# Sums of squares of an SSD chunk: folded to one block of 128 columns, and taken two chunks later by one matmul

## The chip, the cores and the metric

One core of one Trainium2 chip runs the whole program. The time is device microseconds (us) of one execution; lower is better. The kernel before was run three times: 2429.6, 2432.8 and 2435.5 us, median 2432.8.

## What is computed

One layer of a hybrid recurrent decoder for a prompt of 1,024 tokens behind 16 meta tokens, and eight samples of 4 tokens. One of its two branches is a state-space scan (SSD), run in chunks of 128 tokens, with 32 heads of 64 features in 4 groups. Its output is gated and then normalised over the 512 features of a group:

```python
y = jnp.concatenate(ys, axis=1) + w['D'].astype(f32)[:, None] * xs.astype(f32)
y = y.reshape(Bsz, L, S_INNER) * jax.nn.silu(z.astype(f32))
yg = y.reshape(Bsz, L, S_GROUPS, S_INNER // S_GROUPS)
yg = yg * lax.rsqrt(jnp.mean(jnp.square(yg), -1, keepdims=True) + RMS_EPS)
```

The change concerns `jnp.mean(jnp.square(yg), -1)`: for each token, a sum of squares over 512 features.

## The kernel before, in words

**Layout.** In the SSD stage features lie on the 128 partitions and tokens along the columns. A chunk of one group is a tile `xc` of 128 x 10 x 128: four blocks of 128 features of x, then B, C, and four blocks of the gate z. The first chunk has 48 tokens (samples and meta tokens), the eight others 128.

**Order of the work.** `ssd(g)` returns the steps of one group: `first`; `sample` and `sample_states` for the samples' states, twice; for each chunk c `ahead(c)` (store chunk c - 1, load chunk c + 2, `begin(c + 1)`) and `end(c)`; then `norm`. `chained` puts the four groups one behind another, with the next group's `first` ahead of the last two steps. `weave` issues these steps with a priority raised by 60 (`RAHEAD`), and between them 42 pieces of independent matrix products (8 gates and 6 projections, three column ranges each; lines L178 to L180). Within each engine the order is static: a planner settles it when the program is built, by priority and by its own costs and ready times. Each engine then runs its queue in that order, and an instruction that waits holds up all behind it. Scratch tiles with one tag share a ring of `bufs` buffers, and a new tile waits for the last reader of the one whose buffer it takes. PSUM tiles `rps` are a ring of five banks.

**A chunk, engine by engine.** `begin(c)`: ACT exponentiates the decay into E (L933); POOL applies the causal mask to `dec` (L938); ACT exponentiates it by eight heads (L941); PE transposes x and B (L306) and multiplies B by C (L958); DVE and POOL form `xdt` and `xw` (L950); DVE multiplies `dec` by the product (L959); POOL multiplies x by D (L962). `end(c)`: PE multiplies `xdt` by `dec` (L1026), the state by C (L1036), and forms the state's increment (L1045, kept as `aft`); POOL decays the state (L1046), DVE adds to it (L1048); DVE puts the parts of y together (L1037, L1038), adds D x (L1053) and multiplies by z (L1054). Then ACT writes the squares of the chunk over its z (L1057), POOL adds blocks 2 and 3 onto blocks 0 and 1 (L1058), and `sums(c - 1)` follows, which `issue_after(aft.ins)` keeps behind L1045 of chunk c in PE's queue.

**sums(c)** (L1069 to L1078): for each of the two blocks a matmul with the block as the stationary operand and a column of ones as the moving one, both into column 0 of one PSUM bank (L1074); DVE scales the result into column c of `ve` (L1078). `norm` stores chunk 8, calls `sums(8)`, takes the reciprocal root on DVE, transposes it (L1086) and writes it to memory, from where the next stage reads it.

**yi** (L986, L987) holds what the samples' states give, before PE transposes it (L998). It has a buffer of its own; `tmp` (L1028) is the one-buffer scratch of `end`.

Of the kernel before, what the change touches and what calls it, by code (L numbers as in the profile page):

```python
# [12 lines left out]
AF = mybir.ActivationFunctionType  # L13
ALU = mybir.AluOpType
# [48 lines left out]
def kernel(ctx, tc, I, O):  # L63
    nc = tc.nc
    V, S, G, PE = nc.vector, nc.scalar, nc.gpsimd, nc.tensor
# [13 lines left out]
    def rps():  # L79
        return pr.tile([128, 512], F32, tag="r", name="rps")  # L80
# [22 lines left out]
    ones = const.tile([128, 128], F32, name="ones")  # L103
# [38 lines left out]
    def rsqrt(pool, out, x, shape):  # L142

        ti = pool.tile(shape, I32, tag="rs_i", name="rs_i")
        y = pool.tile(shape, I32, tag="rs_y", name="rs_y")
        a = pool.tile(shape, F32, tag="rs_a", name="rs_a")
        h = pool.tile(shape, F32, tag="rs_h", name="rs_h")
        V.tensor_scalar(ti, x.bitcast(I32), 1, None, op0=ALU.logical_shift_right)
        V.tensor_scalar(y, ti, -1.0, float(0x5F3759DF), op0=ALU.mult, op1=ALU.add)
        V.tensor_scalar(h, x, -0.5, None, op0=ALU.mult)  # L150
        cur = y.bitcast(F32)
        for _ in range(3):
            if shape[1] == 1:
                V.scalar_tensor_tensor(a, cur, cur, h, op0=ALU.mult, op1=ALU.mult)
            else:
                V.tensor_tensor(a, cur, cur, ALU.mult)
                V.tensor_tensor(a, a, h, ALU.mult)
            V.scalar_tensor_tensor(out, a, 1.5, cur, op0=ALU.add, op1=ALU.mult)
            cur = out
# [183 lines left out]
    with ExitStack() as c0:  # L343
# [198 lines left out]
        for R, tk in ((R1, tk1), (R2, tk2)):  # L542
            for c0_, cn in ((0, 1), (1, 4), (5, 4)):
                ps = rps()
                pv = ps[:, 0:480].rearrange("p (c r) -> p c r", r=96)
                for c in range(c0_, c0_ + cn):
                    t0, n = CHUNKS[c]
# [6 lines left out]
                n = CHUNKS[c0_][1]  # L554
# [42 lines left out]
    with ExitStack() as c1:  # L597
        tp = c1.enter_context(tc.tile_pool(name="tp", bufs=1))
        raws = [tp.tile([128, T], F32, name=f"raw{q}") for q in range(4)]
        sums = [tp.tile([128, 1024], F32, name=f"sum{q}") for q in range(2)]  # L600
# [149 lines left out]
    with ExitStack() as c1:  # L750
# [126 lines left out]
        for h in range(4):  # L877
            st = mlstm(h, *qk)
# [23 lines left out]
    with ExitStack() as c2:  # L902
        sp = c2.enter_context(tc.tile_pool(name="sp", bufs=1))

        def stile(shape, tag, bufs=1):
            return sp.tile(shape, F32, tag=tag, name=tag, bufs=bufs)

        def ssd(g):

            st = {}  # L910
# [66 lines left out]
            def sample(r):  # L977


                C = st[0][0][:, 5]  # L980
                yps = rps()
                for j in range(4):
                    t = NMETA + NI * (4 * r + j)
                    PE.matmul(yps[32 * j:32 * j + 32], C[:, t:t + 32], st["s0"][2 * r + j // 2][:, j % 2, :],
                              start=True, stop=True)
                yi = stile([128, 512], "yi")  # L986
                S.copy(yi, yps)  # L987
                st["yi"] = yi
                bsm = sp.tile([96, 4, 128], F32R, name="bsm")
                V.tensor_tensor(bsm, st["bs"][:, None, :].bitcast(F32).to_broadcast([96, 4, 128]),  # L990
                                bm[:, 4 * r:4 * r + 4, None].to_broadcast([96, 4, 128]), ALU.mult)
                st["bsm"] = bsm
# [23 lines left out]
            def end(c):  # L1016
                t0, n = CHUNKS[c]
                if c == 8:
                    store(7)
                xc, dec, xdt, xw, bt_, E = st.pop(c)  # L1020
                x, C, z = xc[:, 0:4, 0:n], xc[:, 5], xc[:, 6:10, 0:n]
                St = st.get("S")
                ips = rps()
                iv = ips[:].rearrange("p (m t) -> p m t", t=128)
                for i in range(8):
                    PE.matmul(iv[(i % 2) * 64:(i % 2) * 64 + 64, i // 2, 0:n], xdt[:n, i, :], dec[:n, i, 0:n],  # L1026
                              start=True, stop=True)
                tmp = stile([128, 512], "tmp").rearrange("p (m t) -> p m t", t=128)  # L1028
                if c == 0:
                    V.tensor_copy(tmp[:, :, 0:NMETA], iv[:, :, 0:NMETA])  # L1030
                    V.tensor_tensor(tmp[:, :, NMETA:n], st["tmp"], iv[:, :, NMETA:n], ALU.add)
                else:
                    eps_ = rps()
                    ev_ = eps_[:].rearrange("p (m t) -> p m t", t=128)
                    for i in range(4):
                        PE.matmul(ev_[:, i, :], St[:, i * 128:(i + 1) * 128], C, start=True, stop=True)  # L1036
                    V.tensor_tensor(tmp, ev_, E, ALU.mult)  # L1037
                    V.tensor_tensor(tmp, tmp, iv, ALU.add)  # L1038
                aps = rps()
                Sn = stile([128, 512], "S", 2)  # L1040
                if c == 0:
                    PE.matmul(aps, bt_[NS:NA], xw[NS:NA].rearrange("p h e -> p (h e)"), start=True, stop=True)
                    S.copy(Sn, aps)
                else:
                    aft = PE.matmul(aps, bt_, xw.rearrange("p h e -> p (h e)"), start=True, stop=True)  # L1045
                    G.tensor_tensor(Sn.rearrange("p (h e) -> p h e", e=64), St.rearrange("p (h e) -> p h e", e=64),  # L1046
                                    sdec[:, g * 8:g * 8 + 8, c - 1:c].to_broadcast([128, 8, 64]), ALU.mult)
                    V.tensor_tensor(Sn, Sn, aps, ALU.add)  # L1048
                st["S"] = Sn
                if c == 8:  # L1050
                    dma(O["pS"][g], Sn)

                V.tensor_tensor(x, x, tmp[:, :, 0:n], ALU.add)  # L1053
                V.tensor_tensor(x, x, z, ALU.mult)  # L1054
                st["y", c] = x
                sq = z
                S.activation(sq, x, AF.Square)  # L1057
                G.tensor_tensor(sq[:, 0:2], sq[:, 0:2], sq[:, 2:4], ALU.add)  # L1058
                st["sq", c] = sq
                if c:  # L1060
                    with tc.issue_after(aft.ins):
                        sums(c - 1)

            def store(c):
                a = CUT if c == 0 else 0
                n = CHUNKS[c][1]
                dma(yd[g, :, c, :, a:n], st.pop(("y", c))[:, :, a:n])

            def sums(c):  # L1069
                n = CHUNKS[c][1]  # L1070
                sq = st.pop(("sq", c))
                sps = rps()
                for i in range(2):
                    PE.matmul(sps[:n, 0:1], sq[:, i], ones[:, 0:1], start=i == 0, stop=i == 1)  # L1074
                if c == 0:
                    st["ve"] = stile([128, 9], "ve", 2)
                    V.memset(st["ve"][:, 0:1], 1.0)
                V.tensor_scalar(st["ve"][:n, c:c + 1], sps[:n, 0:1], 1.0 / 512, 4 * EPS, op0=ALU.mult, op1=ALU.add)  # L1078

            def norm():  # L1080
                store(8)
                sums(8)
                rs = stile([128, 9], "rsd")
                rsqrt(sp, rs, st["ve"], [128, 9])
                tps = rps()
                held.append(PE.transpose(tps[:9, 0:128], rs, ident))  # L1086
                rt = stile([9, 128], "rt")
                V.tensor_copy(rt, tps[:9, 0:128])
                dma(rd[g:g + 1, 0:NA - CUT], rt[0:1, CUT:NA])
                dma(rd[g:g + 1, NA - CUT:TC].rearrange("o (c t) -> (o c) t", t=128), rt[1:9])  # L1090
# [15 lines left out]
            for r in range(2):  # L1106
                steps += [lambda r=r: sample(r), lambda r=r: sample_states(r)]
            for c in range(9):
                if c < 8:
                    steps.append(lambda c=c: ahead(c))  # L1110
                steps.append(lambda c=c: end(c))
# [556 lines left out]
```

## Time and profile before

| | us |
|---|---|
| median of three runs | 2432.8 |
| the profiled execution, its own time | 2426.2 |
| its span | 2424.5 |
| PE busy | 2321.9 (96%) |
| DVE busy | 1754.8 (72%) |
| POOL busy | 896.4 (37%) |
| SSD stage, about 955 to 1331 us of the span | 376 |

The profile is of one execution; its times are counted from the start of the span. PE is TensorE's matmuls, PEld its weight loads, DVE the vector engine, ACT the scalar engine, POOL GpSimd, SP the queue that issues DMAs. Float32 matmuls appear twice in the trace, as two passes with a weight load each. In a row of the timeline the numbers are start and duration in us, xN the number of instructions merged into the row, and a bracket the idle time of that engine just before it, with what ended it. In a row of waits: the sum in us, how many, and the longest.

### The profile page before, as it was taken

How to read it: one execution, taken by the hardware profiler on the slowest of the kernel's cores; microseconds unless marked ns; L12 is line 12 of the kernel's file. 1: busy time of each engine (PE TensorE's matmuls, PEld its weight loads, DVE VectorE, ACT ScalarE, POOL GpSimd, SP SyncE). 2: the span in 40 equal slices, each digit the busy share in tenths (PEclk: the TensorE clock that was granted, in tenths of full speed). 3: DMA queues.
4: the chain of work that ended last, by engine and by line, in shares of the span. 5: the costliest groups of instructions: out<-in, count | busy, mean ns of one | idle time of the engine just before them, and what ended most of it. 6: DMA issues, size and time to landing. Idle time of an engine off the chain costs nothing.

```text
span 2424.5 us, 42512 instructions
## 1 busy us (share of the span) xinstructions
PE 2321.9 (96%) x16127; PEld 2190.6 (90%) x16127; DVE 1754.8 (72%) x2997; ACT 992.2 (41%) x1951; POOL 896.4 (37%) x859
## 2 busy tenths in 40 slices
PE   7999999999999999998898999998999999999996
PEld 6889999999998878776777999998999999999995
DVE  7668887888776776778767654578988888864338
ACT  7234444444444333556444221246444444531111
POOL 0035544555551001655655000053566666500004
PEclk9999999999999999999999999999999999999998
DMA  8143334333425764777765743343222222363121
GB/s 265 44 149 100 109 103 114 105 113 100 131 84 188 246 209 169 251 237 232 240 205 164 234 123 98 106 161 122 98 82 81 82 77 78 99 233 100 47 66 72
DMA packets 218589, 334.28 MB, mean 138 GB/s; under 512 B 64760, under 2 KB 150360, under 8 KB 218384
## 3 DMA queue, kind: packets, MB, share of 16 engines
q1 hardware_dynamic: 218384, 331.56, 43.0%
q8 instruction: 127, 2.08, 0.4%
q14 instruction: 78, 0.64, 0.1%
HBM read 233.62 MB, written 97.87 MB: 137 GB/s over the span
## 4 chain that ended last, share of the span: by engine, by line
PE 42%; DVE 6%; POOL 3%; issue 2%; DMA 2%; ACT 2%; SPq 0%; POOLq 0%; ACTq 0%; DVEq 0%
PE gps L179 5%; PE gps L178 5%; PE gps L180 5%; PE rps L280 4%; PE rps L278 4%; PE rps L279 4%; PE rps L180 3%; PE rps L178 3%; PE rps L179 3%; PE gps L278 2%; PE gps L280 2%; PE gps L279 2%; POOL dec L938 1%; POOL S L1046 1%; DVE x1l L164 1%
## 5 line engine op out<-in xcount | busy, mean ns | idle before, releaser
L163 ACT ACTIVATE whi<-wst 128x1024 fp32r<-128x1024 f32 (+1 forms) x105 | 105.7, 1008 | 359.1 <-PE gps L179 178.4
L179 PE MATMUL gps<-pl,whi 128*128 128x352 f32 (+1 forms) x568 | 192.1, 338 | 4.3 <-DVE pl L313 4.3
L278 PE MATMUL rps<-xh,wf 128*128 128x268 f32 x672 | 192.5, 286 | 0.9 <-ACT X L283 0.9
L178 PE MATMUL gps<-ph,whi 128*128 128x352 f32 (+1 forms) x568 | 190.0, 336 | 2.6 <-ACT ph L312 1.3
L280 PE MATMUL rps<-xh,wf 128*128 128x268 f32 x672 | 192.2, 286 | 0.0
L279 PE MATMUL rps<-xl,wf 128*128 128x268 f32 x672 | 191.7, 285 | 0.0
L180 PE MATMUL gps<-ph,wlo 128*128 128x352 f32 (+1 forms) x568 | 190.7, 336 | 0.1
L164 DVE TENSOR_TENSOR wlo<-wst,whi 128x1024 fp32r<-128x1024 f32 (+1 forms) x105 | 129.5, 1236 | 55.3 <-ACT whi L163 53.2
L164 DVE TENSOR_TENSOR wf<-raw,wf 128x512 fp32r<-128x512 f32 x144 | 135.3, 943 | 11.8 <-ACT wf L163 11.4
L178 PE MATMUL gps<-xh,whi 128*128 128x352 f32 (+3 forms) x408 | 139.7, 342 | 0.2 <-DVE X L294 0.2
L179 PE MATMUL gps<-xl,whi 128*128 128x352 f32 (+3 forms) x408 | 138.7, 340 | 0.0
L180 PE MATMUL gps<-xh,wlo 128*128 128x352 f32 (+3 forms) x408 | 138.3, 339 | 0.0
L279 PE MATMUL rps<-x1l,wf 128*128 128x266 f32 x480 | 137.2, 286 | 0.0
L280 PE MATMUL rps<-x1h,wf 128*128 128x266 f32 x480 | 137.2, 286 | 0.0
L278 PE MATMUL rps<-x1h,wf 128*128 128x266 f32 x480 | 137.2, 286 | 0.0
L278 PEld LDWEIGHTS rps<-xh,wf 128*128 128x128 f32 x672 | 126.5, 188 | 1.3 <-ACT X L283 1.3
L163 ACT ACTIVATE wf<-raw 128x512 fp32r<-128x512 f32 x144 | 90.8, 631 | 89.5 <-PE rps L279 87.6
L279 PEld LDWEIGHTS rps<-xl,wf 128*128 128x128 f32 x672 | 126.6, 188 | 0.0
L280 PEld LDWEIGHTS rps<-xh,wf 128*128 128x128 f32 x672 | 126.3, 188 | 0.0
L179 PEld LDWEIGHTS gps<-pl,whi 128*128 128x128 f32 x568 | 110.6, 195 | 10.5 <-issue 5.2
L178 PEld LDWEIGHTS gps<-ph,whi 128*128 128x128 f32 x568 | 109.5, 193 | 6.4 <-issue 2.5
L180 PEld LDWEIGHTS gps<-ph,wlo 128*128 128x128 f32 x568 | 110.3, 194 | 4.6 <-issue 3.8
(478 smaller groups left out, 8236.4 us busy)
## 6 DMA issues: line engine op xcount, KB each, us to landing
raw<-in_win SPq DMA_DIRECT2D x56, 512.0 KB
xc<-xsd SPq DMA_DIRECT2D x32, 640.0 KB
raw<-in_wup SPq DMA_DIRECT2D x40, 512.0 KB
dec<-btd SPq DMA_DIRECT2D x32, 512.0 KB
xsd<-dst SPq DMA_DIRECT2D x24, 512.0 KB
wst<-in_wout SPq DMA_DIRECT2D x24, 512.0 KB
fd<-mix SPq DMA_DIRECT2D x22, 528.0 KB
raw<-fd SPq DMA_DIRECT2D x22, 528.0 KB
```

What stands on the lines that cost most here:

```text
L163: S.activation(hi, src, AF.Copy)
L164: V.tensor_tensor(lo, src, hi.bitcast(F32), ALU.subtract)
L178: PE.matmul(out, ah, bh, start=start, stop=False)
L179: PE.matmul(out, ah, bl, start=False, stop=False)
L180: PE.matmul(out, al, bh, start=False, stop=stop)
L278: PE.matmul(ps, wh[:, k], a, start=new and k == 0, stop=False, **chk)
L279: PE.matmul(ps, wh[:, k], b, start=False, stop=False, **chk)
L280: PE.matmul(ps, wl[:, k], a, start=False, stop=k == 3, **chk)
L938: G.affine_select(out=dec, in_=dec, pattern=[[0, 8], [1, 128]], compare_op=ALU.is_ge, fill=NEG, base=0, channel_multiplier=-1)
L1046: G.tensor_tensor(Sn.rearrange("p (h e) -> p h e", e=64), St.rearrange("p (h e) -> p h e", e=64), sdec[:, g * 8:g * 8 + 8, c - 1:c].to_bro ...
```

## The change

The squares still go over z and blocks 2 and 3 are still added to blocks 0 and 1. A second POOL addition folds the remaining two blocks into one, into a tile `sq` of its own (a ring of four buffers of 128 x 128). `sums` does one matmul instead of two, and `end(c)` calls it for chunk c - 2 instead of c - 1; `norm` takes the sums of chunk 7 as well as of chunk 8. `yi` gives up its buffer and shares the one of `tmp`.

```diff
-                yi = stile([128, 512], "yi")
+                yi = stile([128, 512], "tmp")
...
-                sq = z
-                S.activation(sq, x, AF.Square)
-                G.tensor_tensor(sq[:, 0:2], sq[:, 0:2], sq[:, 2:4], ALU.add)
-                st["sq", c] = sq
-                if c:
+                S.activation(z, x, AF.Square)
+                G.tensor_tensor(z[:, 0:2], z[:, 0:2], z[:, 2:4], ALU.add)
+                sq = st["sq", c] = stile([128, 128], "sq", 4)[:, 0:n]
+                G.tensor_tensor(sq, z[:, 0], z[:, 1], ALU.add)
+                if c > 1:
                     with tc.issue_after(aft.ins):
-                        sums(c - 1)
+                        sums(c - 2)
...
-                for i in range(2):
-                    PE.matmul(sps[:n, 0:1], sq[:, i], ones[:, 0:1], start=i == 0, stop=i == 1)
+                PE.matmul(sps[:n, 0:1], sq, ones[:, 0:1], start=True, stop=True)
...
             def norm():
                 store(8)
+                sums(7)
                 sums(8)
```

## Rows read from the trace of the kernel before

**Rows 1.** The profile's page: the span, and busy time of PE, DVE and POOL (share of the span, instructions).

```profile
span 2424.5 us, 42512 instructions
PE 2321.9 (96%) x16127; PEld 2190.6 (90%) x16127; DVE 1754.8 (72%) x2997; ACT 992.2 (41%) x1951; POOL 896.4 (37%) x859
```

**Rows 2.** Busy time by engine in the four stretches in which chunks 1 to 8 of a group follow each other (columns: the stretch in us, its length, then each engine's busy time with its instructions, TensorE's granted clock as a share of full speed, DMA share, GB/s).

```profile
985.00:1052.00 67.00, 62.06 (x467) 49.46 (x466) 57.05 (x82) 45.88 (x122) 46.98 (x43) 1.00 0.76 243
1079.00:1143.00 64.00, 57.12 (x425) 45.50 (x423) 53.82 (x76) 42.24 (x113) 43.95 (x48) 1.00 0.74 239
1173.00:1238.00 65.00, 59.52 (x426) 48.28 (x425) 51.40 (x76) 38.31 (x106) 44.25 (x41) 0.95 0.67 208
1265.00:1326.00 61.00, 54.59 (x395) 45.34 (x394) 45.77 (x70) 30.76 (x82) 39.59 (x37) 0.94 0.52 166
```

**Rows 3.** PE's waits in these four stretches, in their order (the first asked up to 1051 us). No others are listed there.

```profile
PE rps L1074 <- POOL xc L1058: 4.2, 5, 1.4
...
PE rps L1074 <- POOL xc L1058: 4.6, 5, 1.8
PE rps L1045 <- DVE xdt L950: 0.2, 1, 0.2
...
PE rps L1074 <- POOL xc L1058: 5.5, 4, 2.1
...
PE rps L1074 <- POOL xc L1058: 6.4, 4, 1.8
```

**Rows 4.** The timeline of the second group from 1086 to 1105 us: squares and additions of chunks 1 and 2 (L1057, L1058), the sums of chunk 1 (L1074 at 1091.81), and `aft` of chunks 3 and 4 (L1045).

```profile
1086.91 1.57 DVE L1054 TENSOR_TENSOR xc<-xc 128x512 f32<-128x512 f32 x1
...
1091.03 0.73 POOL L1058 TENSOR_TENSOR xc<-xc 128x256 f32<-128x256 f32 x1 [0.20 <-ACT xc L1057]
...
1091.81 0.61 PE L1074 MATMUL rps<-ones,xc 128*128 128x1 f32 x4 [1.82 <-POOL xc L1058]
...
1096.43 0.63 ACT L1057 ACTIVATE xc<-xc 128x512 f32<-128x512 f32 x1 [0.55 <-DVE xc L1054]
...
1097.05 1.12 PE L1045 MATMUL rps<-xw,btok 128*128 128x512 f32 x2 [0.19 <-DVE xdt L950]
...
1098.08 0.73 POOL L1058 TENSOR_TENSOR xc<-xc 128x256 f32<-128x256 f32 x1
...
1103.46 1.02 PE L1045 MATMUL rps<-xw,btok 128*128 128x512 f32 x2
```

**Rows 5.** The group of PE instructions of L1074 in the SSD stage on chunks of 128 tokens (xcount | busy us, mean ns of one | idle before, with releaser).

```profile
L1074 PE MATMUL rps<-ones,xc 128*128 128x1 f32 x128 | 19.3, 246 | 23.5 <-POOL xc L1058 23.4
```

**Rows 6.** Busy time and granted clock (the third number from the right) in four short stretches of the third and fourth group.

```profile
1186.50:1190.00 3.50, 3.50 (x19) 3.09 (x19) 2.38 (x3) 2.10 (x7) 2.97 (x4) 0.51 0.48 138
1210.40:1213.80 3.40, 3.40 (x23) 3.07 (x20) 3.22 (x4) 1.30 (x5) 3.40 (x3) 0.50 0.89 276
1278.60:1282.00 3.40, 3.40 (x26) 3.10 (x24) 2.87 (x6) 2.58 (x9) 3.40 (x3) 0.51 0.37 101
1316.20:1319.70 3.50, 3.50 (x22) 3.12 (x23) 1.32 (x3) 0.63 (x1) 0.72 (x1) 0.51 0.50 149
```

**Rows 7.** Groups of POOL's additions of L1058, shapes apart (columns as in rows 5).

```profile
L1058 POOL TENSOR_TENSOR xc<-xc 128x256 f32<-128x256 f32 x32 | 24.9, 778 | 33.0 <-ACT xc L1057 33.0
L1058 POOL TENSOR_TENSOR xc<-xc 128x96 f32<-128x96 f32 x4 | 1.8, 460 | 1.6 <-ACT xc L1057 1.6
```

**Rows 8.** The timeline in the fourth group, after POOL's last work of the chunks: DVE's L1054 of chunk 8.

```profile
1324.18 0.69 DVE L1054 TENSOR_TENSOR xc<-xc 128x512 f32<-128x512 f32 x1
```

**Rows 9.** The timeline: the sums of chunk 8 of the first and of the second group, called by `norm`.

```profile
1051.85 0.61 PE L1074 MATMUL rps<-ones,xc 128*128 128x1 f32 x4 [0.57 <-POOL xc L1058]
...
1143.11 0.61 PE L1074 MATMUL rps<-ones,xc 128*128 128x1 f32 x4 [2.20 <-POOL xc L1058]
```

**Rows 10.** The timeline at the first boundary between groups: the last reader of `tmp` (L1053 of chunk 8) and the next group's first copy into `yi`.

```profile
1046.93 1.56 DVE L1053 TENSOR_TENSOR xc<-xc,tmp 128x512 f32<-128x512 f32 x1
...
1056.46 0.59 ACT L987 COPY yi<-rps 128x512 f32<-128x512 f32 x1 [1.96 <-PE rps L984]
```

**Rows 11.** Waits of the whole SSD stage, all engines, that the argument uses.

```profile
ACT dec L941 <- POOL dec L938: 41.4, 24, 3.7
POOL xc L1058 <- ACT xc L1057: 34.5, 23, 7.1
...
DVE tmp L1037 <- PE rps L1036: 18.6, 21, 3.6
...
DVE dec L959 <- ACT dec L941: 14.7, 13, 2.1
```

**Rows 12.** The timeline: `dec` made ready by DVE (L959) and its first use by PE (L1026), for chunks 1 and 3 of the first group and chunk 8 of the last (32 such pairs in all).

```profile
987.60 1.22 DVE L959 TENSOR_TENSOR dec<-dec,rps 128x1024 f32<-128x1024 f32 x1
989.71 1.09 PE L1026 MATMUL rps<-dec,xdt 128*64 128x128 f32 x16
...
1002.95 1.21 DVE L959 TENSOR_TENSOR dec<-dec,rps 128x1024 f32<-128x1024 f32 x1
1004.36 1.09 PE L1026 MATMUL rps<-dec,xdt 128*64 128x128 f32 x16
...
1313.95 1.22 DVE L959 TENSOR_TENSOR dec<-dec,rps 128x1024 f32<-128x1024 f32 x1 [0.43 <-ACT dec L941]
1318.29 1.74 PE L1026 MATMUL rps<-dec,xdt 128*64 128x128 f32 x16
```

## The prediction

> **What bounds the kernel now.** First the page: PE is busy 2321.9 of 2424.5 us, 96% [rows 1], so time can come only from PE's idle time or from work taken off PE. Then the SSD stage, where the change lies, stretch by stretch [rows 2]: in the four stretches in which chunks 1 to 8 follow each other PE is busy 233.3 of 257 us and DVE 208.0 (85, 84, 79 and 75%). So PE leads and DVE is close behind, closest in the first two groups. Then what PE waits for there [rows 3]: POOL's addition of the squares, 4.2 + 4.6 + 5.5 + 6.4 = 20.7 us, and 0.2 us for anything else. The timeline shows why [rows 4]: the sums of chunk 1 reach PE's head and stand there 1.82 us until POOL has ended its addition of that chunk at 1091.76. What stands behind it in PE's queue, independent products and the next chunk's transposes among it, waits as well.
>
> **The change part by part.** The sums are worked out against the profiled execution's own 2426.2 us, 0.3% (6.6 us) under the median of the runs; the gain is then taken off the median.
>
> *Sums one chunk later: the waits.* POOL's addition of chunk 2 ends at 1098.81 (1098.08 + 0.73); the sums of chunk 2 now follow L1045 of chunk 4, which starts at 1103.46 [rows 4]. Even with 0.5 us for the added addition the squares are there 4 us early. All 20.7 us of waits [rows 3] can go. The sums of chunk 8 are not helped: `norm` takes them as directly as before, and the 0.57 and 2.20 us of the first two groups [rows 9] stay.
>
> *One matmul instead of two.* A call is four passes of 0.61 us in all [rows 4], 0.15 us a pass; their long single durations of 246 ns [rows 5] overlap. Two passes go in each of 36 calls: 36 x 0.30 = 10.8 us of PE time, 2.7 us a group. The Trainium skill prices them lower: TensorE: Matmul & The Clock Gate, section Back-to-back issue gap, gives some 81 ns for each pair of weight load and matmul in a sustained stream at 128 columns, by which 72 passes would be an estimated 5.8 us. The float32 pairs of this trace take nearly twice that, and the measurement decides.
>
> *Clock.* In four stretches of 3.4 to 3.5 us in the third and fourth group the granted clock is 0.50 to 0.51, the lower level of 1.2 GHz, with PE busy throughout [rows 6]. The third and fourth groups are those in which PE had idled most before the sums [rows 3]. Each such stretch costs half its length, 1.7 us; without the waits these 6.8 us should go too. Gross gain: 20.7 + 10.8 + 6.8 = 38.3 us.
>
> *The second POOL addition, 128 x 128.* No row has it. The nearest are 460 ns for 128 x 96 and 778 ns for 128 x 256 [rows 7]; these are its bounds, and by the line between them it is 0.52 us. I take 0.5, since 128 is nearer to 96. 36 of them are 18 us (bounds 17 to 28) on POOL, which is busy 174.8 of 257 us [rows 2]; its idle time covers them as far as no one waits for what stands behind them. It costs DVE something: L1054, with both inputs in SBUF, takes 1.57 us beside a busy POOL [rows 4] and 0.69 us beside an idle one [rows 8]. L1053 and L1054, at 0.69 to 1.57 us each [rows 4, 8, 10], are a quarter or more of DVE's 6.5 us a chunk (208 over 32), so of 18 us a quarter meets them and is lost by about half: 3 us on DVE, 0.75 a group; bounds nothing (POOL's additions fall beside DVE's PSUM reads) and 9 us (all of it beside such instructions).
>
> *norm.* Sums(7) comes on top, in halved form and with its squares long there; sums(8) waits 0.5 us more wherever it waited, in two groups [rows 9], and the last group's norm chain is 0.5 us longer: 1.5 us.
>
> *yi in tmp's buffer.* It must now wait for L1053 of the previous group's chunk 8, which ends at 1048.49; the copy comes at 1056.46 [rows 10]. Eight microseconds cover it: nothing. If they shrank, ACT would stand at the copy with PE's transposes behind it.
>
> *z.* POOL and no longer PE ends the life of a chunk's z. The loads that take over its buffer can only come earlier. The DMAs are the same in number and place: nothing.
>
> *What is late next.* DVE. Without PE's stalls it has to deliver the same work in less time. I let it be busy at most 90% of a stretch, a little over the 85% that it reaches in the busiest of the four [rows 2]. With 0.75 us more work a group the stretches then last at least 64.2, 60.6, 57.9 and 51.7 us instead of 67, 64, 65 and 61. Gross, the groups could give 6.9, 7.3, 11.6 and 12.5 us (waits, 2.7 of passes, and 3.4 of clock in the last two); DVE lets through 2.8, 3.4, 7.1 and 9.3, together 22.6. Less norm's 1.5: a gain of 21 us, 2405 on the profiled execution and **2412 us** on the median. With DVE held at 87% the caps are 0.6, 1.3, 5.1 and 7.5, together 13 after norm; at 95% the caps are 6.2, 6.6, 10.1 and 12.0, together 33.4 after norm. The likeliest case's own range is 2399 to 2420.
>
> **The rivals.**
>
> *Nothing caps it.* DVE's waits for PE's L1036 alone are 18.6 us [rows 11], so DVE's lateness is partly PE's own doing; then DVE packs tighter, and all but norm's 1.5 of 38.3 us comes through: 2396. Against it: DVE's share in the first two groups.
>
> *The wait moves to `dec`.* PE needs `dec` from DVE for L1026. It was ready 0.89 us ahead in the first of 32 such pairs, 0.20 us in the tightest and 3.12 us in the last [rows 12]. A PE that comes 0.6 us a chunk earlier (20.7 over 32) has used up such a lead within a few chunks, and from then on goes at the pace of the chain of POOL's mask, ACT's eight exponentials and DVE's product, which the change does not shorten. Waits and clock dips come back one for one at L1026, and PE's saved passes only lengthen them: 2430 to 2433. For it: ACT waits 41.4 us for POOL's mask and DVE 14.7 us for ACT's exponentials [rows 11]. Against it: part of that chain waits for PE.
>
> *Slower: POOL sets the pace.* In POOL's queue the masks of later chunks stand behind these additions. POOL has already been held up 34.5 us at L1058 for ACT's squares [rows 11]; after each such wait the new 0.5 us pushes the mask back, and through it `dec` and L1026. If `dec` becomes what PE waits for, as in the case above, and every mask stands behind one addition, all 32 come through: 16 + 1.5 us, 2450. It decides once POOL's queue, some 5.5 us a chunk (44 us for eight [rows 2]) and then 6.0, has no idle time ahead of a mask. Against it: POOL is idle 30% of these stretches. The Trainium skill, GPSIMD Engine Reference, section Key points, says besides that GpSimd shares its SBUF interfaces with VectorE and contends with instructions of two SBUF inputs; the 1.57 against 0.69 us bear that out, and it would add to the same case.
>
> *It does not do what it says.* The planner arranges each queue anew by its own costs. If it puts the sums later but other recurrence work less well, gain and loss can cancel: around 2433.
>
> **How the numbers follow.** Forecast 0.55, no cap 0.15, wait moved to `dec` 0.15, POOL's pace 0.10, rearrangement 0.05. A measurement of this kernel tells about 0.2% (5 us) from no change. Faster by more than that (under 2428): the first two and a little of the third and the last, 0.73. Within it: most of the third and part of the last, 0.13. Slower: POOL's pace, and the unlucky ends of the other two, 0.14. The range from 2396 to 2435 takes in the forecast, the edge of the uncapped case and the unchanged one; it leaves out most of the slower case and half of the uncapped one.
>
> **What would show it.** Right: L1074 twice a call instead of four times, with hardly a wait in front of it save in norm; DVE's share up to about 90% in the first two groups; the granted clock at 1.0 in most of the third and fourth; the four stretches shorter by 3 to 9 us each, the later groups more. Wrong: waits of some 20 us at L1026 for `dec`, or ACT's wait for POOL's mask well over 41.4 us; POOL's new addition over 0.8 us; the stretches shortened alike by 9 us, which would say that DVE was no cap.

## The result and the profile after

The changed kernel takes 2419.6 us (median of 7 runs, 2414.1 to 2425.0) against 2432.8 before (7 runs in the same comparisons): ratio 0.9946, 95% interval [0.9933, 0.9959], a gain of 13 us where 21 had been forecast. The profiled executions stand 9.1 us apart in span, 2415.4 against 2424.5 [rows 1].

The page of the changed kernel: span and busy time.

```profile
span 2415.4 us, 42442 instructions
PE 2311.3 (96%) x16055; PEld 2180.5 (90%) x16055; DVE 1758.8 (73%) x2997; ACT 991.5 (41%) x1951; POOL 910.4 (38%) x895
```

PE has 72 instructions and 10.6 us less, DVE 4 us more with the same instructions, POOL 14 us more with 36 additions. PE is still at 96%. Its 10.6 us are more than the 9.1 us by which the span fell: over the whole execution PE stands idle for 104.1 us, against 102.6 before. Taken as a sum, its idle time did not shrink. What the later sums did by themselves only the experiments can tell.

PE's waits in the SSD stage of the changed kernel (920 to 1345 us; sum in us, how many, longest). L1073 is the sums' matmul, L1059 the new POOL addition.

```profile
PE rps L1073 <- POOL sq L1059: 6.1, 5, 2.7
PE rps L306 <- DMA xc<-xsd: 5.6, 5, 2.3
...
PE rps L1073 <- ACT btok L955: 3.7, 2, 1.9
PE rps L306 <- DVE dec L959: 3.1, 3, 2.2
...
PE rps L984 <- DMA s<-in_s0T: 1.8, 2, 1.0
```

The 20.7 us of waits for POOL [rows 3] are gone. The 6.1 us that are left at L1073 belong to the sums of the last two chunks of a group, taken in `norm` (2.67 us in the second group, 2.20 before [rows 9]). In their place stand waits that the chunks did not have before: the transposes of L306 wait for loads, and L306 and the sums wait for a PSUM bank that an ACT or DVE instruction has to read first.

Busy time and granted clock of the four stretches of chunks (columns as in [rows 2], whose counterparts these are; the borders follow the groups, which begin earlier each time).

```profile
985.00:1052.00 67.00, 62.16 (x462) 49.83 (x460) 58.18 (x83) 44.22 (x119) 50.65 (x50) 1.00 0.80 250
1079.00:1142.00 63.00, 55.62 (x404) 44.31 (x403) 53.65 (x77) 44.08 (x116) 48.60 (x56) 0.97 0.78 247
1173.00:1232.00 59.00, 54.40 (x390) 43.01 (x390) 49.13 (x72) 38.07 (x101) 45.70 (x46) 1.00 0.72 228
1260.00:1315.00 55.00, 50.75 (x370) 41.71 (x366) 45.85 (x68) 30.33 (x79) 43.24 (x45) 0.97 0.57 179
```

DVE is busy 87, 85, 83 and 83% of them. These stretches end 1 to 3 us farther behind L1026 of chunk 8 than those of [rows 2]; from the first L1026 of chunk 1 to the end of chunk 8's, DVE is busy 89, 85, 87 and 84%, against 86, 85, 78 and 76% before. The clock is up from 0.95 and 0.94 to 1.00 and 0.97 in the last two, and down from 1.00 to 0.97 in the second. From the first L1026 of a group to its last one the timeline gives 54.3, 56.0, 54.6 and 51.2 us, 1.9, 1.9, 5.6 and 6.8 us less than before: the later groups gained most, as forecast, and each gained between a half and four fifths of its forecast. The sums of the four stretches from the first L1026 of chunk 1 to the end of chunk 8's split the gain (before, changed, and the kernel `delay_only` of the experiments; first number: length, then busy time by engine).

```profile
sum 216.60, PE 195.74 PEld 156.18 DVE 175.76 ACT 129.34 POOL 158.39; mean PE 48.94 PEld 39.04 DVE 43.94 ACT 32.34 POOL 39.60
```

```profile
sum 200.40, PE 184.41 PEld 145.18 DVE 172.61 ACT 127.86 POOL 170.36; mean PE 46.10 PEld 36.29 DVE 43.15 ACT 31.96 POOL 42.59
```

```profile
sum 197.10, PE 188.01 PEld 151.31 DVE 180.44 ACT 128.40 POOL 158.52; mean PE 47.00 PEld 37.83 DVE 45.11 ACT 32.10 POOL 39.63
```

Between chunks 1 and 8 PE's idle time went from 20.9 us to 16.0, and to 9.1 with the later sums alone; the rest of the 16.2 us by which the stretches are shorter is PE's busy time, down by 11.3.

Where some of PE's new waits come from is seen in the fourth group (timeline, chain picked out).

```profile
1282.71 0.79 POOL L1059 TENSOR_TENSOR sq<-xc 128x128 f32<-128x128 f32 x1
...
1284.97 2.08 DVE L164 TENSOR_TENSOR wlo<-wst,whi 128x1024 fp32r<-128x1024 f32 x1
...
1285.92 2.08 POOL L938 TENSOR_SCALAR_AFFINE_SELECT dec<-dec 128x1024 f32<-128x1024 f32 x1
...
1288.04 0.99 ACT L941 ACTIVATE dec<-dec,tk 128x128 f32<-128x128 f32 x3 [3.15 <-POOL dec L938]
1288.93 0.61 ACT L1056 ACTIVATE xc<-xc 128x512 f32<-128x512 f32 x1
1289.45 1.55 ACT L941 ACTIVATE dec<-dec,tk 128x128 f32<-128x128 f32 x5
...
1291.11 1.22 DVE L959 TENSOR_TENSOR dec<-dec,rps 128x1024 f32<-128x1024 f32 x1 [2.67 <-ACT dec L941]
...
1292.38 0.45 PE L306 MATMUL rps<-ident,xc 128*128 128x128 f32 x1 [2.19 <-DVE dec L959]
```

From 1276.8 on POOL works without a pause, and it comes to the mask at 1285.92. ACT has stood 3.15 us for it, DVE 2.67 us for ACT's exponentials, and PE's transpose gets its bank when L959 has read it, at 1292.33. The new addition has 0.79 us of this chain; the mask itself, beside DVE's L164, took 2.08 us. Over the stage ACT waits 48.2 us for the mask and DVE 16.2 us for the exponentials (41.4 and 14.7 before [rows 11]).

In the second group the addition stands directly ahead of a mask, and the sums stand for the bank of B's transpose, which ACT reads (L955) behind its exponentials.

```profile
1091.27 1.33 POOL L1059 TENSOR_TENSOR sq<-xc 128x128 f32<-128x128 f32 x1
1092.56 1.54 POOL L938 TENSOR_SCALAR_AFFINE_SELECT dec<-dec 128x1024 f32<-128x1024 f32 x1
...
1094.13 2.44 ACT L941 ACTIVATE dec<-dec,tk 128x128 f32<-128x128 f32 x8 [3.13 <-POOL dec L938]
1096.48 0.24 ACT L955 COPY btok<-rps 128x128 f32<-128x128 f32 x1
...
1096.87 0.35 PE L1073 MATMUL rps<-ones,sq 128*128 128x1 f32 x2 [1.88 <-ACT btok L955]
```

There is a second path, through the loads. The new addition reads z, and so it ends the life of a chunk's buffer (waits of the DMA queue, 930 to 1345 us, then the timeline of the third group).

```profile
SPq L918 <- POOL sq L1059: 13.2, 9, 2.4
```

```profile
1202.76 0.90 POOL L1059 TENSOR_TENSOR sq<-xc 128x128 f32<-128x128 f32 x1
...
1203.69 0.32 SPq L918 DMA_DIRECT2D xc<-xsd  x1
...
1208.29 0.63 PE L306 MATMUL rps<-ident,xc 128*128 128x128 f32 x4 [2.26 <-DMA xc<-xsd]
```

Nine loads wait for it in SP's queue. Behind two of them PE stands for 2.07 and 2.26 us, most of its 5.6 us of waits for loads. Before the change the loads stood longer, 29.8 us for PE's sums (L1074), and PE waited for none of them. Now it comes earlier, and the loads do not: from chunk 4 of a group on they are issued 0.9 us later than before, counted from L1026 of the chunk two ahead.

### The profile page after: what moved, and what is told of

Same layout as the page of the kernel before. It is cut to its first block, busy times and chain, and to the rows that moved or that the text cites. A ratio compares the mean times of both kernels' runs of the same rounds, so it can differ in the third digit from the quotient of the medians.

```text
span 2415.4 us, 42442 instructions
## 1 busy us (share of the span) xinstructions
PE 2311.3 (96%) x16055; PEld 2180.5 (90%) x16055; DVE 1758.8 (73%) x2997; ACT 991.5 (41%) x1951; POOL 910.4 (38%) x895
## 4 chain that ended last, share of the span: by engine, by line
PE 69%; DVE 10%; DMA 4%; ACT 4%; POOL 4%; issue 3%; SPq 0%; POOLq 0%; DVEq 0%; ACTq 0%
PE rps L278 9%; PE rps L280 9%; PE rps L279 9%; PE gps L179 6%; PE gps L180 6%; PE gps L178 6%; PE gps L278 3%; PE gps L280 3%; PE gps L279 3%; PE rps L180 3%; PE rps L178 3%; PE rps L179 3%; ACT dec L941 1%; DVE cv L652 1%; POOL dec L938 1%
## 5 line engine op out<-in xcount | busy, mean ns | idle before, releaser
L178 PE MATMUL gps<-ph,whi 128*128 128x352 f32 (+1 forms) x568 | 188.6, 335 | 1.3 <-ACT whi L163 1.3
L180 PE MATMUL gps<-ph,wlo 128*128 128x352 f32 (+1 forms) x568 | 189.0, 333 | 0.2
L164 DVE TENSOR_TENSOR wlo<-wst,whi 128x1024 fp32r<-128x1024 f32 (+1 forms) x105 | 130.5, 1246 | 56.3 <-ACT whi L163 55.5
L164 DVE TENSOR_TENSOR wf<-raw,wf 128x512 fp32r<-128x512 f32 x144 | 138.0, 962 | 12.1 <-ACT wf L163 11.4
L178 PE MATMUL gps<-xh,whi 128*128 128x352 f32 (+3 forms) x408 | 138.8, 340 | 0.1
L180 PE MATMUL gps<-xh,wlo 128*128 128x352 f32 (+3 forms) x408 | 137.3, 337 | 0.0
L178 PEld LDWEIGHTS gps<-ph,whi 128*128 128x128 f32 x568 | 109.3, 193 | 5.6 <-issue 3.2
L180 PEld LDWEIGHTS gps<-ph,wlo 128*128 128x128 f32 x568 | 109.6, 193 | 3.0 <-issue 2.1
```

What stands on the lines that cost most here:

```text
L164: V.tensor_tensor(lo, src, hi.bitcast(F32), ALU.subtract)
L178: PE.matmul(out, ah, bh, start=start, stop=False)
L180: PE.matmul(out, al, bh, start=False, stop=stop)
```

## The experiments

All were timed against the kernel before on the same chip, but not all on one chip, so ratios are compared rather than times. half_sums, no_d and no_sums leave a part of the work out of the result. *PE idle* is 405 us less PE's busy time between 940 and 1345 us; *mask* is ACT's wait for L938, *exponentials* DVE's wait for L941; *stage* is the time from the first L1026 of the first group to the end of the last one of the fourth. These four are of one profiled execution each, which lies within some 4 us of the kernel's median, but 6.6 us below it for the kernel before and 9 us above it for fold_only. Before the stage and behind it, where the work is nearly the same, these executions differ by 6 and 7 us among themselves.

| kernel | sums | matmuls | POOL additions | median us | ratio to before [95%] | PE idle | mask | exponentials | stage |
|---|---|---|---|---|---|---|---|---|---|
| before | c - 1 | 2 | 1 | 2432 | 1 | 39 | 41 | 15 | 334.3 |
| changed | c - 2 | 1 | 2 | 2419.6 | 0.9946 [0.9933, 0.9959] | 37 | 48 | 16 | 320.8 |
| fold_only | c - 1 | 1 | 2 | 2435.0 | 1.0011 [0.9998, 1.0023] | 48 | 35 | 7 | 344.3 |
| delay_only | c - 2 | 2 | 1 | 2407.7 | 0.9907 [0.9892, 0.9922] | 27 | 43 | 8 | 314.6 |
| half_sums | c - 2 | 1 | 1 | 2409.7 | 0.9906 [0.9892, 0.9920] | 32 | 41 | 8 | 312.1 |
| delay_add | c - 2 | 2 | 2 | 2412.7 | 0.9923 [0.9909, 0.9937] | 31 | 50 | 13 | 322.0 |
| pool_twice | c - 2 | 1 | 3 | 2429.2 | 0.9996 [0.9985, 1.0007] | 46 | 58 | 16 | 333.2 |
| no_d | c - 2 | 1 | 2 | 2407.7 | 0.9902 [0.9886, 0.9919] | 30 | 35 | 6 | 309.8 |

**fold_only**: the single matmul and the second addition without the later sums.

```diff
-                if c > 1:
+                if c:
                     with tc.issue_after(aft.ins):
-                        sums(c - 2)
+                        sums(c - 1)
...
-                sums(7)
```

> The changed kernel with the sums taken one chunk later again, as before the change; the second POOL addition, the single matmul and yi in tmp's buffer stay. Theory A (the gain is the PE work saved, 72 passes at 0.15 us = 10.8 us, and the waits only moved): 8 to 12 us under the kernel before, 2421 to 2425, with PE's waits for the POOL addition at the sums 20 to 35 us. Theory B (the forecast: the gain comes mainly from the waits taken away, capped by DVE): without the later sums the waits stay and grow by 0.5 us a chunk, so at most 3 us under before, 2430 to 2440.

Theory B's outcome. PE's wait at the sums, from its waits between 930 and 1345 us:

```profile
PE rps L1073 <- POOL sq L1059: 29.1, 21, 3.0
```

It grew from 23.4 us [rows 5], and the saved passes, with the addition's cost beside them, bought nothing. Theory A, that the gain was the saved PE work, fell here as an account by itself; half_sums below takes the matmul alone.

**delay_only**: the later sums without the rest.

```diff
-                G.tensor_tensor(z[:, 0:2], z[:, 0:2], z[:, 2:4], ALU.add)
-                sq = st["sq", c] = stile([128, 128], "sq", 4)[:, 0:n]
-                G.tensor_tensor(sq, z[:, 0], z[:, 1], ALU.add)
+                sq = st["sq", c] = stile([128, 2, 128], "sq", 3)[:, :, 0:n]
+                G.tensor_tensor(sq, z[:, 0:2], z[:, 2:4], ALU.add)
...
-                PE.matmul(sps[:n, 0:1], sq, ones[:, 0:1], start=True, stop=True)
+                for i in range(2):
+                    PE.matmul(sps[:n, 0:1], sq[:, i], ones[:, 0:1], start=i == 0, stop=i == 1)
```

> The sums two chunks later, but with two matmuls as before the change and without the second POOL addition: POOL writes the sum of the two halves of the squares into a tile of its own, 256 columns, three buffers. yi stays in tmp's buffer. Theory A: 0 to 4 us under before, 2429 to 2433, with PE waiting elsewhere, at L306 and at the sums for a PSUM bank, about as long as it did for POOL. Theory B: the waits' part of the gain, 10 to 15 us, 2418 to 2423.

More than either theory had: 22 to 24 us, and 10 to 12 us under the changed kernel. It beats both kernels. ("The later sums alone" here takes in the addition into a tile of its own and yi in tmp's buffer.) PE's busy time over the stage in it, in the changed kernel and in the kernel before (columns as in [rows 2], first number behind the stretch's length):

```profile
940.00:1345.00 405.00, 377.87 (x2589) 312.26 (x2589) 301.79 (x474) 209.16 (x517) 223.19 (x212) 0.97 0.71 232
```

```profile
940.00:1345.00 405.00, 368.20 (x2482) 300.69 (x2482) 292.46 (x471) 205.32 (x514) 241.12 (x248) 0.96 0.71 228
```

```profile
940.00:1345.00 405.00, 365.90 (x2472) 297.80 (x2473) 282.30 (x460) 202.05 (x510) 222.21 (x212) 0.95 0.67 219
```

In the same 405 us PE is busy 12 us longer in delay_only than in the kernel before, and 2.3 us longer in the changed kernel. DVE, busy 282.3 us there before, is busy 301.8. Between the L1026 of chunks 1 and 8 (columns as in [rows 2]) it is busy 89, 91, 94 and 93%, more than the 90% at which the forecast had capped it:

```profile
990.30:1039.40 49.10, 47.01 (x369) 37.15 (x368) 43.52 (x61) 33.48 (x93) 42.09 (x37) 1.00 0.75 245
1077.00:1128.00 51.00, 48.28 (x368) 38.97 (x367) 46.60 (x62) 33.94 (x89) 39.00 (x43) 0.97 0.79 248
1166.90:1215.40 48.50, 46.52 (x364) 36.85 (x363) 45.45 (x62) 31.48 (x88) 40.05 (x37) 1.00 0.75 240
1252.40:1300.90 48.50, 46.20 (x364) 38.34 (x364) 44.87 (x61) 29.49 (x79) 37.38 (x34) 1.00 0.59 190
```

Its waits in the mask's chain:

```profile
ACT dec L941 <- POOL dec L938: 43.2, 31, 2.9
...
DVE dec L959 <- ACT dec L941: 8.1, 10, 1.7
```

From these two runs came theory C: what the later sums win, the second addition takes back in part by standing in POOL's queue ahead of the masks.

**half_sums and delay_add** take the other two edits one at a time, on top of delay_only.

```diff
-                for i in range(2):
-                    PE.matmul(sps[:n, 0:1], sq[:, i], ones[:, 0:1], start=i == 0, stop=i == 1)
+                PE.matmul(sps[:n, 0:1], sq[:, 0], ones[:, 0:1], start=True, stop=True)
```

> The kernel with delay alone and one matmul instead of two, without a second addition: the second half of the squares is left out of the sums. It is the saved matmul by itself. If PE's work sets the time of the stage: 72 passes at 0.15 us, 8 to 12 us under delay alone, 2396 to 2400. If the chain of mask, exponentials and product sets it: 0 to 4 us under it, 2404 to 2408.

```diff
                 G.tensor_tensor(sq, z[:, 0:2], z[:, 2:4], ALU.add)
+                G.tensor_tensor(z[:, 0], sq[:, 0], sq[:, 1], ALU.add)
```

> The kernel with delay alone (two matmuls, sums two chunks later), with one further POOL addition of 128 x 128 behind the existing one, its result unused. It is the second addition without the saved matmul. Theory C (the addition delays the masks and is what ate the gain): 10 to 22 us over delay alone, 2418 to 2430, ACT's wait for the mask from 43 to 48 us or more, PE idle in the SSD stage from 27 to 36 us. If a rearranged plan and not the addition made the difference: within 4 us of delay alone, 2404 to 2412.

The saved matmul is worth nothing that these runs can tell: 0.9906 against 0.9907, where 10.8 us would be 0.0044; the two intervals leave room for some 5 us. Half_sums has 5 us more PE idle time in the window instead:

```profile
940.00:1345.00 405.00, 372.99 (x2530) 304.55 (x2529) 303.41 (x484) 208.61 (x517) 221.62 (x212) 0.98 0.72 234
```

Its stage is 2.5 us shorter than delay_only's. 711 of the independent products' matmuls (L178 to L180) start in it, against 725, so 14 of them, an estimated 3 us at the 0.2 us that one takes there, now stand behind it; and PE's idle time in it is 23.1 us against 17.5. These three parts add up to about the 10.8 us.

The addition by itself costs some 4 us (0.0016; the intervals overlap, so its size is uncertain), with the waits that theory C names: mask 50.3 us and exponentials 13.4 us against 43.2 and 8.1. This lies between the two expected outcomes, so theory C's price was missed. The two together cost 10 to 12 us (the changed kernel against delay_only), more than the two apart; the stages, 2.5 us shorter, 7.4 longer and 6.2 longer with both, show no such excess. Whether the two act on each other is not shown.

**pool_twice** and **no_d** change POOL's load alone, from the changed kernel.

```diff
                 G.tensor_tensor(sq, z[:, 0], z[:, 1], ALU.add)
+                G.tensor_tensor(sq, z[:, 0], z[:, 1], ALU.add)
```

> The changed kernel with the second POOL addition done twice into the same tile: 36 further additions of 128 x 128, 17 us of POOL. If POOL's time is hidden (the forecast took 3 us of 18 through DVE): 0 to 4 us over the changed kernel, 2420 to 2424. If POOL's queue, by the masks behind these additions, paces the stage and so ate the rest of the gain: 10 to 18 us over it, 2430 to 2438, with ACT's wait for POOL's mask over 55 us (48.2 in the changed kernel).

```diff
-                G.tensor_tensor(x, x, Dc[:, 4 * g:4 * g + 4, None].to_broadcast([128, 4, n]), ALU.mult)
```

> The changed kernel without POOL's multiplication of x by D (L962), so D is left out of the result: 36 instructions of 1.0 to 1.5 us, some 41 us less POOL in the SSD stage, nothing added elsewhere. Theory C (POOL's queue, by the masks behind its other work, paces the changed kernel): 12 to 25 us under the changed kernel, 2395 to 2408, with ACT's wait for the mask well under 48 us and PE idle in the stage at 25 us or less. If POOL does not pace it (DVE's share, the PSUM banks or the order of the plan do): within 6 us of it, 2414 to 2424.

A third addition costs another 10 to 12 us, at the lower edge of what theory C expected; 41 us of POOL work less bring 11 or 12 back, at the upper edge of its times and with 30 us of PE idle time, not 25. Waits of pool_twice, then of no_d:

```profile
ACT dec L941 <- POOL dec L938: 57.8, 31, 3.5
...
DVE dec L959 <- ACT dec L941: 15.8, 13, 2.7
```

```profile
ACT dec L941 <- POOL dec L938: 34.7, 29, 3.6
...
DVE dec L959 <- ACT dec L941: 5.8, 6, 1.4
```

With the load ACT's wait for the mask goes from 34.7 over 48.2 to 57.8 us, the stage from 309.8 over 320.8 to 333.2, and the time from 2407.7 over 2419.6 to 2429.2. POOL's work is thus on the path of the changed kernel, at a price between a quarter (no_d) and more than half (pool_twice) of its own length. How much of it goes by the masks and how much by the loads, which wait 17.4 us for the last addition in pool_twice, was not separated. DVE's slowing beside POOL can be only a small part of it: DVE's busy time over the execution is 1757.0, 1758.8 and 1762.1 us in these three, and 1765.1 in the faster delay_only.

ACT's wait for the mask is a sign of POOL's lateness only among kernels that are alike otherwise: fold_only has both additions and waits 35 us, no more than no_d, while PE stands at the sums.

**dve_fold** moves the second addition to DVE.

```diff
-                G.tensor_tensor(sq, z[:, 0], z[:, 1], ALU.add)
+                V.tensor_tensor(sq, z[:, 0], z[:, 1], ALU.add)
```

> The changed kernel with the second addition on DVE instead of POOL; single matmul and two chunks' delay stay. Theory C (what the later sums win, the second addition takes back by standing in POOL's queue ahead of the causal masks, on which ACT's exponentials, DVE's product and at last the PSUM banks wait): 10 to 18 us under the changed kernel, 2402 to 2410, with ACT's wait for the mask back at some 43 us and PE's idle time in the SSD stage at 27 us or less (36 in the changed kernel). Theory B (DVE's share is the cap): 36 x 0.28 us more on DVE, so 0 to 10 us over the changed kernel, 2420 to 2430.

2424.5 us, ratio 0.9969 [0.9956, 0.9982]: 5 us slower than the changed kernel, so theory C's time was missed and theory B's (0 to 10 us over) met. Its waits show both sides:

```profile
ACT dec L941 <- POOL dec L938: 35.8, 26, 2.8
...
DVE sq L1059 <- POOL xc L1057: 23.3, 27, 1.8
```

The mask came earlier, but DVE now stands for POOL's first addition, with the parts of y behind it in its queue: one wait was exchanged for another. The run says little of DVE's share, which delay_only has shown not to be the cap.

**late_adds, delay_late, one_bank, delay_three.** The additions issued one chunk later (in the changed kernel and in delay_only), six banks a chunk instead of seven, the sums three chunks later.

```diff
+                st["z", c] = z
+                if c:
+                    fold(c - 1)
```

> The changed kernel with both POOL additions of a chunk issued one chunk later, so that POOL does not stand at them waiting for ACT's squares; same work, same sums. Theory C: POOL's waits of 28.4 us at L1057 go, ACT's wait for the mask falls under 40 us, and the time is 5 to 15 us under the changed kernel, 2405 to 2415. If it is POOL's work and not its waiting that delays the masks: within 3 us of the changed kernel.

> The kernel with delay alone (two matmuls, one POOL addition into a tile of its own, sums two chunks later), and that addition issued one chunk later. Theory C: again 3 to 10 us under the kernel with delay alone, 2398 to 2405. If waiting is not what delays the masks: within 3 us of it, 2405 to 2411.

```diff
                 bps = rps()
+                cps = bps[:, 128:256]
...
-                cps = rps()
```

> The changed kernel with B's transpose and the product of B and C in one PSUM bank instead of two, so six allocations a chunk instead of seven in the ring of five; both written before either is read. If the number of banks is what PE waits for at L306 and at the sums: PE's idle time in the SSD stage falls from 36 to 28 us or less, and the time is 5 to 12 us under the changed kernel, 2408 to 2415. Theory C (the late mask chain, whatever the bank): within 4 us of it, the waits moving to L1026.

```diff
-                if c > 1:
+                if c > 2:
...
-                        sums(c - 2)
+                        sums(c - 3)
```

> The changed kernel with the sums three chunks later instead of two; the same work. Its squares are ready long before either way, so this shows how much a plan that the change leaves arbitrary moves the time: theory C expects 0 to 4 us from the changed kernel, 2416 to 2424. If lateness of the sums still cost something at two chunks: 5 to 10 us under it.

late_adds: 2418.5 us, 0.9934 [0.9918, 0.9951]; delay_late: 2406.6, 0.9886 [0.9866, 0.9906]. Neither tested what it was made for: POOL runs its instructions in the same order as in the changed kernel and in delay_only, and its wait for the squares stayed at 27.8 us in late_adds (28.4 in the changed kernel). They can be read as repeats of those two kernels, and as such they bear out the 10 to 12 us between them.

```profile
POOL xc L1066 <- ACT xc L1056: 27.8, 21, 4.3
```

one_bank: 2420.3, 0.9943 [0.9924, 0.9962]: one bank less a chunk brings nothing, as theory C expected. It also frees the shared bank only after the later of two readers, so by itself it does not rule out the number of banks as a limit. delay_three: 2418.5, 0.9950 [0.9938, 0.9962]: two chunks are late enough. The medians of late_adds, delay_three and the changed kernel, the same work in two orders, lie within 2 us.

**no_sums** drops the sums' matmuls, their bank and DVE's scaling.

```diff
-                sps = rps()
-                PE.matmul(sps[:n, 0:1], sq, ones[:, 0:1], start=True, stop=True)
...
-                    V.memset(st["ve"][:, 0:1], 1.0)
-                V.tensor_scalar(st["ve"][:n, c:c + 1], sps[:n, 0:1], 1.0 / 512, 4 * EPS, op0=ALU.mult, op1=ALU.add)
+                    V.memset(st["ve"], 1.0)
```

> The changed kernel without the sums' matmuls, their PSUM bank and DVE's scaling of them; the reciprocal root is taken of ones, so the normalisation is left out; squares and POOL additions stay. If only PE work counts (theory A): the other 72 passes at 0.15 us, 10.8 us, and the waits of the groups' last sums, some 5 us: 15 us under the changed kernel, 2405. If PE's new waits come from the ring of five PSUM banks (one of seven allocations a chunk goes), PE's waits at L306 fall well under their present 10 us too, and it is 20 us or more under it, 2400. Theory B (DVE is the cap): 5 us or less under it, since DVE keeps its work but for 36 x 0.15 us.

All expectations were missed: 2426.4 us, 0.9972 [0.9960, 0.9984], slower than the changed kernel with less work. Its PE waits:

```profile
PE rps L984 <- DMA s<-in_s0T: 10.8, 3, 5.0
PE rps L1026 <- DVE dec L959: 7.5, 4, 5.1
```

In its plan the recurrence runs ahead of a state load and of `dec`, with fewer of the independent products to cover it: 671 of their matmuls start in the stage, 714 in the changed kernel. That this order, and not something else, costs the 7 us was not tried by itself. It does warn that the planner's answer to an edit can be worth several us, as much as some of the differences above; no run holds the order fixed while the addition's length changes.

## Why the prediction was right, and where its sum was not

*Waits.* Right for the later sums alone: they bring 22 to 24 us (delay_only), against 20.7 of waits and 6.8 of clock forecast gross, and without them the other edits bring nothing (fold_only). In the changed kernel part of the waits came back in other places: PE's idle time between chunks 1 and 8 is 16.0 us, against 20.9 before and 9.1 in delay_only.

*One matmul instead of two.* Mis-sized: forecast at 10.8 us, measured at nothing that can be told (half_sums). PE's busy time went, 10.6 us over the execution, but in half_sums it came back as idle time and as independent products that moved behind the stage. The Trainium skill's lower price (TensorE: Matmul & The Clock Gate, section Back-to-back issue gap), by which the forecast estimated 5.8 us, is for 128 moving columns; these matmuls have one. It would have been nearer, but the miss is not in the price of a pass: saved PE time did not become saved time here.

*Clock.* Right in direction, half in size: the third and fourth stretch rose to 1.00 and 0.97, but the second fell to 0.97. Of four stretches of 3.4 us at the lower level two are left, one of them new in the second group, so some 3.4 of the 6.8 us came.

*The second addition.* Its duration was right (0.57 us measured, 0.5 taken). DVE's extra time, 4 us where 3 had been forecast, cannot be put down to it: DVE is busy 10 us longer than before in delay_only, which does not have the addition, and 1 us longer in delay_add, which has it. Its cost was not right: the sum took only DVE's part, but standing in POOL's queue it delays the masks and the loads; 4 us by itself, 10 to 12 us with the single matmul, and 10 to 12 for one more. That is the mechanism of the slower rival; its condition held in part, its price was paid in part, and the later sums outweighed it.

*norm.* PE's waits for the last chunks' sums went from 2.8 us [rows 9] to 6.1: 3.3 us where 1.0 had been put down for them. The sums of chunk 7, which no edge holds back in `norm`, waited too, 0.86 us in the first group (L1073 at 1045.93), where their squares had been taken to be long there.

*yi in tmp's buffer.* Nothing was seen of it, as forecast, but it was not undone alone.

*z.* Put at nothing, since the loads could only come earlier. They came 0.9 us later, nine of them behind POOL's second addition, and PE, which comes earlier, waits 5.6 us for loads where it had waited for none (2.7 us in delay_only).

*What is late next.* This is the step that failed. DVE's share was not the cap: it stayed at 83 to 87% in the changed kernel, and delay_only drives it to 91, 94 and 93% in three of four groups at a better time. What came late next was, for some 8 of PE's 16.0 us of waits between chunks 1 and 8, POOL's mask, ACT's exponentials and copy and DVE's product in their order, and behind them the PSUM banks: the second rival's chain, met at L306 and the sums and hardly at L1026 (1.0 us). The forecast's own sign for it, ACT's wait for the mask well over 41.4 us, came at 48.2. For another 5.6 us it was the loads. That the cap gave a number near the truth (21 us for 13) was luck: it cut a gross gain that contained 10.8 us of passes which did not come, and it stood in for a cost on POOL that the sum had put at nothing.

## What to carry to other kernels

Taking a wait off the busiest engine pays for as long as no in-order chain stands right behind it; ask then which queue that chain passes, and count what the change puts into it. Here a cheap addition on an engine that had been busy 68% of the stretches cost more than the matmul that it saved brought, with masks and loads waiting behind it. Take an edit apart before keeping it whole: the later sums alone were 10 to 12 us better than the change as made.

## What the runs showed of the hardware

A 128 x 128 float32 addition took 0.57 us on POOL in the mean, 0.45 us at its shortest and 1.33 us at its longest, and one of 128 x 48 took 0.29 us:

```profile
L1059 POOL TENSOR_TENSOR sq<-xc 128x128 f32<-128x128 f32 x32 | 18.1, 565 | 2.4
...
L1059 POOL TENSOR_TENSOR sq<-xc 128x48 f32<-128x48 f32 x4 | 1.1, 286 | 0.3
```

POOL's mask of 128 x 1024 took 1.10 us in the row below, and 2.08 us in the chain shown above, beside a DVE instruction that reads both inputs from SBUF:

```profile
1292.85 1.10 POOL L938 TENSOR_SCALAR_AFFINE_SELECT dec<-dec 128x1024 f32<-128x1024 f32 x1
```
